# FFN up products by Strassen's algorithm in a two-layer diffusion step: seven block products in place of eight

## The chip, the cores and the metric

The kernel runs on 1 core of one Trainium2 chip. The metric is the device time of one execution in microseconds (us), taken as the median of several runs. PE is the matrix engine, DVE the vector engine, ACT the scalar engine, POOL the GpSimd engine, SP the engine whose queue issues most DMAs. SBUF is the on-chip memory that all engines read and write; PE writes its results to PSUM, which the code divides into buffers ("banks") of 512 fp32 columns and from which DVE and ACT read.

## What is computed

One inference step of two layers (shared structure, own weights) over 1152 tokens (128 context tokens, then 1024 latent ones) of width 1024. Each layer is a token mixer (three kinds of attention with one input and one output projection) and a gated convolutional FFN, each between norms whose scale, shift and gate (adaLN) are products of the conditioning vectors. What the change touches is the FFN:

```python
def conv_ffn(h, w_up, conv_w, conv_b, w_down):
    u = h @ w_up
    up = jnp.pad(u, ((0, 0), (1, 1), (0, 0)))
    u = up[:, :-2] * conv_w[0] + up[:, 1:-1] * conv_w[1] + up[:, 2:] * conv_w[2] + conv_b
    gate, val = jnp.split(u, 2, axis=-1)
    return (jax.nn.silu(gate) * val) @ w_down
...
    x = x + gt_m * rms_norm(o, g_post_mix)
    h = rms_norm(x, g_pre_ffn) * (1 + sc_f) + sh_f
    x = x + gt_f * rms_norm(conv_ffn(h, ffn_w_up, ffn_conv_w, ffn_conv_b, ffn_w_down), g_post_ffn)
```

`w_up` is 1024 x 5632, `w_down` 2816 x 1024. The context and the latent tokens are two sequences for the convolution.

## The kernel before

The tokens are nine tiles of 128. Every large product is of fp32 values in three passes: a value x is split into hi, rounded by a cast, and lo = x - hi (`split`, L195), and PE adds hi·hi, hi·lo and lo·hi. The cast is ACT's, the subtraction POOL's or DVE's. The tile framework schedules the instructions from the order in which the code issues them; each engine then runs its list in order and waits on semaphores. Buffers are taken from pools: a tag has a number of buffers, and a new tile waits for the last use of the buffer it gets; a pool that is opened in the room of an old one waits for that.

A layer has five stages. `phase_a` (L363) is the input projection, `phase_b` (L621) the attention, with its scores at L679 and its values at L727. `phase_c` (L944, stage C) is the output projection (L968), then per tile the norms (`norm_tiles`, L158: the product with the gate row at L166, the reciprocal root by Newton steps at L106 to L121, the scaling at L188) and the transposed, modulated and split h (`h_group`, L139) in groups of one to three tiles.

`phase_u` (L989, stage U) runs over 22 pairs f of a gate and a value block of 128 features. `load_w` (L342) loads a block of 512 KB, ACT casts it and POOL subtracts. `up_mm` (L998) makes the block in three PSUM banks: 8 slices of the 1024 input features, 3 passes, 3 chunks of 384 tokens, 72 matmuls, so 144 per f. The convolution of width 3 is applied to the blocks straight from PSUM: ACT writes the centre tap and the bias into `acc` (L1040), DVE adds the two shifted taps, with the product in PSUM as one input (`shifted`, L1015; 16 operations, since tokens are interleaved in groups of eight and chunks have edges). ACT applies SiLU to the gate (L1078), POOL multiplies gate and value (L1053), SP stores the result to DRAM (`GT`). For f = 0 the products of chunks 0 and 1 come first, 96 matmuls, since the last tiles' h is not there yet; `pend` holds the generators of the last norms.

Beside U's products `along` (L1056) advances a generator: `ada_dve` (L297), the adaLN products of this layer's last part and, in layer 0, of all the next layer's, as vector operations on DVE (L311, 512 wide) with a transpose on PE and a reduction (L321). U is followed by the class `Down` (L1095): per group of three tiles 22 blocks of `w_down`, loaded three ahead, 512-column matmuls into six banks (L1120). Its norms, one per tile, go along.

## Time and profile before

| | us |
|---|---|
| median of 3 runs | 3373.86 (3371.49 to 3375.37) |
| profiled execution, its own time | 3374.83 |
| its span in the profile | 3373.0 |
| PE busy | 3209.3 (95%) |
| DVE busy | 2165.7 (64%) |
| ACT busy | 1546.9 (46%) |
| POOL busy | 1127.5 (33%) |

The span runs from the first to the last instruction that the profile has; the device time has 1.8 us around it. Busy is the time in which an engine had an instruction at work; a busy PE is not necessarily PE at its peak. In rows of the timeline, consecutive instructions of a kind stand together with their count (x16), and a time in brackets is what the engine stood idle before them, with what ended that.

### The profile page before, as it was taken

The numbers are of one execution on the slowest core, as the hardware profiler recorded it, in microseconds if no ns is written. First come the engines' busy times: TensorE is split into PE (matmuls) and PEld (weight loads), VectorE is DVE, ScalarE is ACT, GpSimd is POOL, SyncE is SP. The second block draws the span as 40 slices with busy tenths as digits, with TensorE's granted clock in tenths as the row PEclk, the third lists the DMA queues.
The fourth block names the chain that finished last, engine by engine and source line by source line (L and its number), as shares of the span: only waits on it lengthen the run. The fifth ranks groups of instructions, "written<-read, shape, count | busy, mean of one in ns | idle before, by whom it ended". The sixth has DMA issues, their size and how long they took to land.

```text
span 3373.0 us, 51130 instructions
## 1 busy us (share of the span) xinstructions
PE 3209.3 (95%) x18068; PEld 2895.7 (86%) x18068; DVE 2165.7 (64%) x5367; ACT 1546.9 (46%) x3209; POOL 1127.5 (33%) x962
## 2 busy tenths in 40 slices
PE   8988999989999999999999899999899999999999
PEld 3868888877899999987788699888779999999887
DVE  5796788877788888435546728888777433333443
ACT  4321688875332222235544228888643222223443
POOL 2122345431233323344421314554313332323443
PEclk9999999999999999999999999999999999999999
DMA  6467431253243333255544563215423221123665
GB/s 238 132 182 224 140 77 40 66 168 132 80 140 123 122 120 120 79 187 191 192 137 126 150 189 87 59 41 133 158 94 100 87 73 65 65 69 118 207 204 167
DMA packets 224863, 428.78 MB, mean 127 GB/s; under 512 B 21088, under 2 KB 127456, under 8 KB 224608
## 3 DMA queue, kind: packets, MB, share of 16 engines
q1 hardware_dynamic: 223312, 424.33, 40.9%
q8 instruction: 143, 2.34, 0.3%
q10 hardware_dynamic: 1296, 1.19, 0.1%
q14 instruction: 112, 0.92, 0.1%
HBM read 324.05 MB, written 101.38 MB: 126 GB/s over the span
## 4 chain that ended last, share of the span: by engine, by line
PE 71%; DVE 13%; ACT 7%; issue 4%; DMA 3%; POOL 1%; SPq 0%; ACTq 0%; DVEq 0%; POOLq 0%
PE mm L1003 32%; PE mm L1120 15%; PE O L727 5%; PE T L709 4%; PE mm L968 4%; PE SA L679 4%; ACT P L689 3%; PE mm L591 2%; DVE PT L206 2%; ACT PT L205 2%; PE mm L375 1%; PE mm L376 1%; PE mm L374 1%; DVE nw_t L116 1%; PE SB L679 1%
## 5 line engine op out<-in xcount | busy, mean ns | idle before, releaser
L1003 PE MATMUL mm<-hhi,wu 128*128 128x384 f32 x4224 | 863.4, 335 | 3.1 <-POOL wu L200 2.2
L1003 PEld LDWEIGHTS mm<-hhi,wu 128*128 128x128 f32 x4224 | 742.7, 188 | 4.3 <-POOL wu L200 2.8
L1015 DVE SCALAR_TENSOR_TENSOR acc<-mm,conv,acc 128x336 f32<-128x336 f32 (+6 forms) x1408 | 412.5, 375 | 314.8 <-ACT acc L1040 314.5
L200 POOL TENSOR_TENSOR wu<-wraw,wu 128x1024 fp32r<-128x1024 f32 x123 | 302.2, 2458 | 690.3 <-ACT wu L197 690.2
L1003 PE MATMUL mm<-hlo,wu 128*128 128x384 f32 x2112 | 490.9, 334 | 0.0
L197 ACT CAST wu<-wraw 128x1024 fp32r<-128x1024 f32 x158 | 165.7, 1051 | 593.6 <-issue 369.6
L1003 PEld LDWEIGHTS mm<-hlo,wu 128*128 128x128 f32 x2112 | 377.1, 188 | 0.6 <-DVE hlo L153 0.4
L727 PE MATMUL O<-PT,V 128*128 128x256 f32 (+1 forms) x1936 | 334.4, 299 | 22.6 <-ACT PT L205 10.5
L698 POOL TENSOR_SCALAR P<-P,rs 128x1152 f32<-128x1152 f32 (+3 forms) x288 | 273.2, 950 | 185.5 <-DVE rs L697 123.0
L709 PE MATMUL T<-ident,P 128*128 128x128 f32 x1832 | 292.8, 278 | 16.5 <-DVE PT L206 12.3
L311 DVE SCALAR_TENSOR_TENSOR aacc<-wadv,sc,aacc 128x512 f32<-128x512 f32 x280 | 261.2, 976 | 63.5 <-DMA wadv<-w_ada 63.3
L206 DVE TENSOR_TENSOR PT<-T,PT 128x512 fp32r<-128x512 f32 (+1 forms) x448 | 284.4, 650 | 23.9 <-ACT PT L205 18.9
L727 PEld LDWEIGHTS O<-PT,V 128*128 128x128 f32 x1936 | 263.1, 192 | 40.2 <-ACT PT L205 16.7
L679 PE MATMUL SA<-k,q 128*128 128x256 f32 (+5 forms) x1224 | 283.8, 353 | 9.2 <-ACT ko L616 4.0
L1120 PE MATMUL mm<-wd,g 128*128 128x512 f32 x1224 | 288.1, 392 | 2.6 <-DVE wt L166 2.6
L1120 PEld LDWEIGHTS mm<-wd,g 128*128 128x128 f32 x1224 | 230.2, 189 | 51.4 <-DVE wt L166 3.5
L1120 PE MATMUL mm<-wu,g 128*128 128x512 f32 x1152 | 270.7, 391 | 2.6 <-DVE wt L166 2.6
L205 ACT CAST PT<-T 128x512 fp32r<-128x512 f32 (+1 forms) x448 | 241.9, 563 | 58.3 <-PE T L709 46.3
L1120 PEld LDWEIGHTS mm<-wu,g 128*128 128x128 f32 x1152 | 216.4, 188 | 48.2 <-DVE wt L166 3.5
L709 PEld LDWEIGHTS T<-ident,P 128*128 128x128 f32 x1832 | 210.4, 141 | 50.2 <-issue 17.6
L679 PEld LDWEIGHTS SA<-k,q 128*128 128x128 f32 (+1 forms) x1224 | 199.0, 193 | 32.9 <-ACT P L689 6.8
L702 DVE TENSOR_REDUCE mx<-SA 128x1 f32<-128x896 f32 (+1 forms) x192 | 182.4, 950 | 36.6 <-PE SA L679 36.6
(203 smaller groups left out, 5033.4 us busy)
## 6 DMA issues: line engine op xcount, KB each, us to landing
wraw<-w_down SPq DMA_DIRECT2D x132, 512.0 KB, 3.6
wraw<-w_up SPq DMA_DIRECT2D x88, 512.0 KB, 3.6
wadv<-w_ada SPq DMA_DIRECT2D x160, 256.0 KB, 3.0
GT<-acc SPq DMA_DIRECT2D x44, 576.0 KB, 3.0
graw<-GT SPq DMA_DIRECT2D x132, 192.0 KB, 3.1
...
```

Of the source, the lines that this page charges most:

```text
L200: (lo_eng or pool).tensor_tensor(out=lo, in0=raw, in1=hi.bitcast(F32), op=ALU.subtract)
L205: act.copy(hi, src)
L206: dve.tensor_tensor(out=lo, in0=src, in1=hi.bitcast(F32), op=ALU.subtract)
L311: dve.scalar_tensor_tensor(out=accs[i], in0=w, scalar=sc[:, k, i:i + 1], in1=accs[i], op0=ALU.mult, op1=ALU.add)
L679: pe.matmul(out, q[0:rows, qc:qc + 128], kview(k[0:rows]), start=(i == 0), stop=(i == len(passes) - 1))
L698: pool.tensor_scalar(out=P[:, :n], in0=P[:, :n], scalar1=rs, scalar2=1.0, op0=ALU.mult, op1=ALU.mult)
L702: dve.tensor_reduce(out=out, in_=src, op=ALU.max, axis=AX.X, negate=True)
L709: pe.transpose(tp[:, j * 128:(j + 1) * 128], p, ident)
L727: pe.matmul(op[0][:, c0:c1], V[:, vt, :], PT[e][:, sl, c0:c1], start=(i == 0 and e == 0), stop=(i == last and e == 1))
L1003: pe.matmul(pts[c][:, :CN], a[:, k, :], h_[:, k, c * CN:(c + 1) * CN], start=(k == 0 and a is whi and h_ is hhi), stop=(k == KC - 1 and a ...
L1015: dve.scalar_tensor_tensor(out=d, in0=src, scalar=w, in1=d, op0=ALU.mult, op1=ALU.add)
L1120: pe.matmul(pts[j], a[:, ts], d[:, 0, j * 512:(j + 1) * 512], start=(f == 0 and n == 0), stop=(f == NFF - 1 and n == 2))
```

## The change

For each f the products A·B, with A the two blocks (rows gate and value, columns the two halves of the 1024 input features) and B = h (rows the two halves of the features, columns the two halves of the tokens, 576 each), are made by the Strassen-Winograd scheme of seven products:

- of the weights: S1 = A21 + A22, S2 = S1 - A11, S3 = A11 - A21, S4 = A12 - S2 (class `Up`, `step`): S1 and S3 on POOL, S2 and S4 on DVE, 512 wide; the seven hi parts on ACT, the seven lo parts on POOL;
- of h: T3 = B22 - B12, T2 = T3 + B11, T1 = B22 - T2, T4 = B21 - T2, made once per layer (class `Halves`, `h_of`), tile by tile; T1, T4 and B22 go through DRAM;
- seven products A11·B11, A12·B21, S2·T2, S3·T3, A22·T4, S1·T1, S4·B22, each of 4 slices, 3 passes and 2 halves of 288 tokens: 24 matmuls, 168 per f, into a pair of PSUM banks `mm2` (three pairs);
- seven additions on DVE of a product in PSUM to a sum in SBUF (`add`, L1211), and a copy on ACT, which make `C0` (gate) and `C1` (value) in SBUF. The convolution's inputs are then both in SBUF (L1184): 8 operations of 1008, 112 and 15 elements per block. Gate and value of f - 1 are finished in f.

Besides: f = 0 has only A11·B11 and A12·B21 before it needs the last tile's h; `phase_c` has two pools of single buffers that alternate by tile, and h comes tile by tile (`SINGLE`); adaLN products are 256 wide, six steps per f, in U only this layer's last part and the next layer's first two parts, and the other three go along layer 0's Down (two steps per block); `Down` loads three ahead in the last layer and two in the first, `w_down` in two halves, the first two loads in U's buffers; the rope table and a gain row are loaded in `phase_a`; every pool has `reuse_waits="tile"`: a new tile waits for the last users of the tiles whose room it takes, and not for the whole old pool.

The diff, cut to its core:

```diff
-    const = ctx.enter_context(tc.tile_pool(name="const", bufs=1))
...
+    const = ctx.enter_context(tc.tile_pool(reuse_waits="tile", name="const", bufs=1))
...
+    def mm2():
+        return psum.tile([128, 1024], F32, name="mm2", tag="mm2", bufs=3)
...
+        (st0, p0), (st1, p1) = right("cp0"), right("cp1")
+        junk = p0.tile([128, 512], BF16, name="junk")
+        G = [gate_rows(z, 0, 0, p0.tile([128, D], F32, name="G")),
+             gate_rows(z, 0, 1, p1.tile([128, D], F32, name="G1"))]
...
+            xt = load_x(p, xin, t, "xt", 1)
+            wt = p.tile([128, D], F32, name="wt")
+            gens.append(norm_tiles(p, (t,), [pts.pop(t)], [[junk] * 2], [wt], [xt], G, xout, z.Af,
+                                   z.mods[:, 3], H, xs, SINGLE, (dve, dve), T.h_of))
...
+    HF, HT = KC // 2, NT // 2
...
+                B12, B22, B11, B21 = hr[:, 0:HF, n0:], hr[:, HF:KC, n0:], hs[:, 0:HF], hs[:, HF:KC]
+                dve.tensor_tensor(out=B12, in0=B22, in1=B12, op=ALU.subtract)
+                self.split("T3", r, B12)
+                dve.tensor_tensor(out=B11, in0=B12, in1=B11, op=ALU.add)
+                self.split("T2", r, B11)
+                pool.tensor_tensor(out=t1, in0=B22, in1=B11, op=ALU.subtract)
+                pool.tensor_tensor(out=B21, in0=B21, in1=B11, op=ALU.subtract)
...
+            self.raw = lambda n: p.tile([128, 1024], F32, name=n, bufs=1 if n == "A1" else 2)
+            self.sum = lambda n: p.tile([128, 512], F32, name=n)
+            self.hi = lambda n: p.tile([128, 512], F32R, name="h" + n)
+            self.lo = lambda n: p.tile([128, 512], F32R, name="l" + n)
...
+            if i == 0:
+                comb("S1", "A21", "A22", ALU.add, pool)
+                comb("S3", "A11", "A21", ALU.subtract, pool)
+                hi("A11")
+            elif i == 1:
+                comb("S2", "S1", "A11", ALU.subtract, dve)
+                lo("A11")
+                hi("A12")
+            elif i == 2:
+                comb("S4", "A12", "S2", ALU.subtract, dve)
+                lo("A12")
+                hi("S2")
+                lo("S2")
+            else:
+                n = ("S3", "A22", "S1", "S4")[i - 3]
+                hi(n)
+                lo(n)
+
+    def phase_u(l, z, T, W, p, up, pend, pend_done):
+
...
+        def product(s, t, f):
+            (shi, slo), (thi, tlo) = W.f[f][s], T.parts[t]
+            acc = mm2()
+            for k in range(HF):
+                for n, (a, b) in enumerate(((shi, thi), (shi, tlo), (slo, thi))):
+                    for j in range(2):
+                        pe.matmul(acc[:, j * 512:j * 512 + 288], a[:, k * 128:(k + 1) * 128],
+                                  b[:, k, j * 288:(j + 1) * 288], start=(k == 0 and n == 0),
+                                  stop=(k == HF - 1 and n == 2))
+            return acc
...
+            def add(d0, s0, n, te, fe):
+                d = dst[:, d0:d0 + n, te]
+                dve.scalar_tensor_tensor(out=d, in0=src[:, s0:s0 + n, fe], scalar=w, in1=d,
+                                         op0=ALU.mult, op1=ALU.add)
+
+            if sh == 1:
+                add(0, 0, 144, slice(1, 8), slice(0, 7))
+                add(1, 0, 15, 0, 7)
+                add(32, 16, 112, 0, 7)
+                add(17, 128, 15, 0, 7)
+            else:
+                add(0, 0, 144, slice(0, 7), slice(1, 8))
+                add(0, 1, 15, 7, 0)
+                add(16, 32, 112, 7, 0)
+                add(128, 17, 15, 7, 0)
+
...
+            act.activation(out=acc, in_=C, func=AF.Identity, scale=cw[:, 1:2], bias=cw[:, 3:4])
...
+            u2 = up.tile([128, HT], F32, name="U2")
+            a = product("A11", "B11", f)
+            act.copy(two(u2), view(a))
+            if f:
+                W.step(f, 6)
+                W.load(f + 1)
+                prep(0)
+                ag = conv(Cg, f - 1, 0)
+                act.activation(out=ag, in_=ag, func=AF.Silu)
+                pool.tensor_tensor(out=av, in0=ag, in1=av, op=ALU.mult)
+                nc.sync.dma_start(out=GT[l][f - 1], in_=av)
+                add(Cg[:, 0:HT], u2, product("A12", "B21", f))
+                prep(1)
+                along(2)
+                add(u2, u2, product("S2", "T2", f))
+                prep(2)
+                add(Cv[:, HT:], u2, product("S3", "T3", f))
             else:
...
+                a = product("A12", "B21", f)
                 for g in list(pend):
                     finish(g, pend)
+                T.from_last()
                 p, extra = pend_done()
-                up_mm(wg, pg, (2,))
-                up_mm(wv, pv_, (2,))
-            else:
-                up_mm(wg, pg, range(NCH))
-            ag = conv(pg, f, 0)
-            act.activation(out=ag, in_=ag, func=AF.Silu)
-            along()
-            if f > 0:
-                wv = load_up(f + NFF)
-                pv_ = [mm() for _ in range(NCH)]
-                up_mm(wv, pv_, range(NCH))
...
+            prep(3)
+            along(2)
+            add(Cv[:, 0:HT], Cv[:, HT:], product("A22", "T4", f))
+            prep(4)
+            a = product("S1", "T1", f)
+            add(Cv[:, HT:], Cv[:, HT:], a)
+            add(u2, u2, a)
+            prep(5)
+            av = conv(Cv, f + NFF, 1)
+            add(Cg[:, HT:], u2, product("S4", "B22", f))
+            along(2)
+        ag = conv(Cg, f, 0)
...
-                    self.load(i0 + f + AHEAD)
+                    self.load(i0 + f + self.bufs - 1)
...
+            ex.append(ada_dve(l, z, p, (5,), 256))
             if zn is not None:
-                ex.append(ada_dve(l + 1, zn, p, (1, 0, 2, 3, 4), 512))
...
+        extra = [] if zn is None else [ada_dve(l + 1, zn, ep, (2, 3, 4), 256)]
...
+        def step():
+            advance(gens)
+            for _ in range(2):
+                advance(extra)
```

What the order of the instructions shows, at three places.

DVE in U of layer 0, within one f. Before: a convolution's end (`mm` is the product in PSUM, `acc` the sum in SBUF), then an adaLN step (`aacc`).

```order
L1015 SCALAR_TENSOR_TENSOR acc_13006<-mm,conv,acc_13006 128x48x7 x2
L1015 SCALAR_TENSOR_TENSOR acc_13006<-mm,conv,acc_13006 128x48
L1015 SCALAR_TENSOR_TENSOR acc_13006<-mm,conv,acc_13006 128x32
L1015 SCALAR_TENSOR_TENSOR acc_13006<-mm,conv,acc_13006 128x15
L1015 SCALAR_TENSOR_TENSOR acc_13006<-mm,conv,acc_13006 128x48x7
L1015 SCALAR_TENSOR_TENSOR acc_13006<-mm,conv,acc_13006 128x48
L311 SCALAR_TENSOR_TENSOR aacc_12801<-wadv,sc,aacc_12801 128x512
L321 TENSOR_REDUCE ada_m<-aux 128x4
```

Now: additions of products (`C`, `U`, `S` and `A` are in SBUF), a weight combination and a convolution between adaLN steps.

```order
L1211 TENSOR_TENSOR C_10712<-C_10712,mm_14129 128x576
L313 SCALAR_TENSOR_TENSOR aacc_14119<-wadv,sc,aacc_14119 128x256
L313 SCALAR_TENSOR_TENSOR aacc_14120<-wadv,sc,aacc_14120 128x256
L313 SCALAR_TENSOR_TENSOR aacc_14119<-wadv,sc,aacc_14119 128x256
L313 SCALAR_TENSOR_TENSOR aacc_14120<-wadv,sc,aacc_14120 128x256
L1211 TENSOR_TENSOR C_10712<-C_10712,mm_14159 128x576
L1211 TENSOR_TENSOR U_13953<-U_13953,mm_14159 128x576
L1125 TENSOR_TENSOR S_14314<-S_14269,A_14265 128x512
L313 SCALAR_TENSOR_TENSOR aacc_14119<-wadv,sc,aacc_14119 128x256
L1184 SCALAR_TENSOR_TENSOR acc_14190<-C_10712,conv,acc_14190 128x144x7
L1184 SCALAR_TENSOR_TENSOR acc_14190<-C_10712,conv,acc_14190 128x15
L1184 SCALAR_TENSOR_TENSOR acc_14190<-C_10712,conv,acc_14190 128x112
```

The convolution reads SBUF twice where it read PSUM and SBUF, and the adaLN operations stand between the additions that free PSUM.

POOL in U, from one product of gate and value to the next. Before, the low parts of two blocks:

```order
L1053 TENSOR_TENSOR acc_12650<-acc_12536,acc_12650 128x1152
L200 TENSOR_TENSOR wu_12927<-wraw,wu_12926 128x1024
L200 TENSOR_TENSOR wu_13041<-wraw,wu_13040 128x1024
L1053 TENSOR_TENSOR acc_12891<-acc_12765,acc_12891 128x1152
```

Now seven low parts (L1133) and two combinations (L1125):

```order
L1225 TENSOR_TENSOR acc_12801<-acc_12894,acc_12801 128x1152
L1133 TENSOR_TENSOR lS_12979<-S_12933,hS_12977 128x512
L1133 TENSOR_TENSOR lS_13009<-S_12890,hS_13007 128x512
L1125 TENSOR_TENSOR S_13161<-A_13155,A_13156 128x512
L1133 TENSOR_TENSOR lA_13047<-A_12885,hA_13045 128x512
L1133 TENSOR_TENSOR lS_13078<-S_12888,hS_13076 128x512
L1125 TENSOR_TENSOR S_13159<-A_13156 128x512
L1133 TENSOR_TENSOR lS_13153<-S_12973,hS_13151 128x512
L1133 TENSOR_TENSOR lA_13206<-A_13155,hA_13163 128x512
L1133 TENSOR_TENSOR lA_13242<-A_13155,hA_13208 128x512
L1225 TENSOR_TENSOR acc_13080<-acc_13165,acc_13080 128x1152
```

Three instructions of POOL per f became ten.

PE at the start of U, layer 0. Before, at the transposes of the last tile's h (`wt`), 96 up products of chunks 0 and 1 lie between these rows and the last output projection:

```order
L1003 MATMUL mm<-hhi,wu_10474 128x384
L1003 MATMUL mm<-hlo,wu_10474 128x384
L1003 MATMUL mm<-hhi,wu_10475 128x384
L148 MATMUL aux<-ident,wt 128x128 x2
L1003 MATMUL mm<-hhi,wu_10465 128x384
```

Now the end of the second product (`hA`, `lA`), the first matmuls of S3·T3 and S2·T2, whose columns are there (`hS`), and the transposes of tile 8:

```order
L1164 MATMUL mm_10676<-hlo,hA_10518 128x288 x2
L1164 MATMUL mm_10676<-hhi,lA_10522 128x288 x2
L1164 MATMUL mm_10730<-hhi,hS_10528 128x288
L1164 MATMUL mm_10755<-hhi,hS_10524 128x288
L1035 MATMUL aux<-ident,wt 128x128 x8
L1164 MATMUL mm_10730<-hhi,hS_10528 128x288
L1164 MATMUL mm_10730<-hlo,hS_10528 128x288
```

Two products of 24 matmuls stand ahead of the transposes, where 96 longer ones did.

## Rows read from the trace of the kernel before

**Rows 1.** Windows: stretch, us; PE, PEld, DVE, ACT, POOL busy (count); PEclk, DMA, GB/s.

```profile
876.00:1442.70 566.70, 563.80 (x3283) 560.71 (x3282) 423.04 (x963) 159.02 (x225) 174.89 (x74) 1.00 0.36 114
1442.70:1760.00 317.30, 307.36 (x1361) 250.83 (x1360) 151.68 (x313) 150.29 (x250) 129.39 (x80) 0.99 0.58 184
2535.00:3092.80 557.80, 554.85 (x3201) 552.14 (x3200) 252.99 (x768) 158.53 (x224) 170.11 (x74) 1.00 0.23 78
```

**Rows 2.** Chain of waits: start us, us, what.

```profile
1442.71 89.82 PE mm L1120 x396
...
2638.33 454.48 PE mm L1003 x2622
```

**Rows 3.** Timeline of PE in attention: start us, us, engine, line, operation, count.

```profile
700.36 0.32 PE L727 MATMUL O<-PT,V 128*128 128x256 f32 x1
...
700.83 1.30 PE L727 MATMUL O<-PT,V 128*128 128x256 f32 x9
```

**Rows 4.** Groups by line and form: busy us, mean ns | idle before.

```profile
L1015 DVE SCALAR_TENSOR_TENSOR acc<-mm,conv,acc 128x336 f32<-128x336 f32 x352 | 190.3, 562 | 0.0
...
L1053 POOL TENSOR_TENSOR acc<-acc,acc 128x1152 f32<-128x1152 f32 x44 | 119.9, 2725 | 199.3 <-DVE acc L1015 176.2 <-issue 16.5 <-DMA wraw<-w_up 6.6
...
L1078 ACT ACTIVATE acc<-acc 128x1152 f32<-128x1152 f32 x44 | 51.5, 1170 | 173.0 <-DVE acc L1015 173.0
...
L166 DVE TENSOR_TENSOR wt<-mm,G 128x512 f32<-128x512 f32 x72 | 48.7, 686 | 39.6 <-ACT wt L127 31.2 <-ACT junk L127 8.3
...
L1015 DVE SCALAR_TENSOR_TENSOR acc<-mm,conv,acc 128x15 f32<-128x15 f32 x176 | 42.8, 243 | 0.0
...
L321 DVE TENSOR_REDUCE ada_m<-aux 128x4 f32<-128x512 f32 x40 | 27.5, 689 | 36.6 <-PE aux L320 36.2
...
L200 POOL TENSOR_TENSOR cv<-cv,cv 128x512 fp32r<-128x512 f32 x2 | 2.6, 1295 | 0.2 <-ACT cv L197 0.2
```

**Rows 5.** Timeline of DVE, in stage C and in U of layer 0.

```profile
857.40 1.29 DVE L166 TENSOR_TENSOR wt<-mm,G 128x512 f32<-128x512 f32 x2 [1.85 <-ACT wt L127]
...
1103.61 4.66 DVE L1015 SCALAR_TENSOR_TENSOR acc<-mm,conv,acc 128x127 f32<-128x127 f32 x16
1108.18 2.73 DVE L311 SCALAR_TENSOR_TENSOR aacc<-wadv,sc,aacc 128x512 f32<-128x512 f32 x4
```

**Rows 6.** Timeline of all engines at 1112 us, in U of layer 0.

```profile
1112.38 4.22 DVE L311 SCALAR_TENSOR_TENSOR aacc<-wadv,sc,aacc 128x512 f32<-128x512 f32 x3 [1.47 <-DMA wadv<-w_ada]
1112.54 2.85 POOL L200 TENSOR_TENSOR wu<-wraw,wu 128x1024 fp32r<-128x1024 f32 x1 [10.07 <-ACT wu L197]
```

**Rows 7.** Timeline of all engines at 1138 us, in U of layer 0.

```profile
1138.38 2.41 POOL L200 TENSOR_TENSOR wu<-wraw,wu 128x1024 fp32r<-128x1024 f32 x1 [10.97 <-ACT wu L197]
...
1138.85 2.29 DVE L1015 SCALAR_TENSOR_TENSOR acc<-mm,conv,acc 128x127 f32<-128x127 f32 x8 [1.59 <-ACT acc L1040]
```

**Rows 8.** Timeline of all engines at 859 us, in stage C of layer 0.

```profile
858.96 4.76 POOL L200 TENSOR_TENSOR wu<-wraw,wu 128x1024 fp32r<-128x1024 f32 x2 [8.91 <-ACT wu L197]
858.98 2.40 DVE L116 SCALAR_TENSOR_TENSOR nw_t<-nw_u,nw_v 128x1 f32<-128x1 f32 x1
...
861.41 2.33 DVE L120 SCALAR_TENSOR_TENSOR nw_u<-nw_t,nw_u 128x1 f32<-128x1 f32 x1
```

**Rows 9.** Timeline at the start of U, layer 0: the last tile's norm.

```profile
876.94 0.68 DVE L166 TENSOR_TENSOR wt<-mm,G 128x512 f32<-128x512 f32 x1
...
886.35 1.15 ACT L188 ACTIVATE wt<-xt,nw_u 128x1024 f32<-128x1024 f32 x1 [1.83 <-DVE nw_u L120]
```

**Rows 10.** DMA issues: KB each, median us from issue to landing.

```profile
GT<-acc SPq DMA_DIRECT2D x44, 576.0 KB, 3.0
```

**Rows 11.** Waits of PE from 730 to 880 us: us in total, times, longest.

```profile
PE O L727 <- DVE Y L734: 3.9, 2, 3.5
PE mm L968 <- ACT hhi L197: 2.0, 1, 2.0
```

More of the change, by code (lines that the diff above doesn't have):

```diff
@@ L38 @@
 GW = 64
+SINGLE = tuple((t,) for t in range(NTT))
 GROUPS = ((0,), (1, 2), (3, 4, 5), (6, 7), (8,))
@@ L165, in norm_tiles @@
             for j, wj in enumerate(halves(w[i])):
-                eng[j].tensor_tensor(out=wj, in0=src[i][j], in1=halves(G[:, 1 if tiles[i] == 0 else 0])[j],
+                eng[j].tensor_tensor(out=wj, in0=src[i][j], in1=halves(G[1 if tiles[i] == 0 else 0])[j],
                                      op=ALU.mult)
@@ L377, in project @@
             return pt
[L380 removed]
+        with tc.tile_pool(reuse_waits="tile", name="av", bufs=1) as p:
             for t in range(NTT):
@@ L1084, in phase_u @@
-            av = conv(pv_, f + NFF, 1)
-            gate(ag, av)
-            along()
+                Cg, Cv = [p.tile([128, NT], F32, name=f"C{j}") for j in range(2)]
+                add(Cg[:, 0:HT], u2, a)
+                W.load(f + 1)
+                prep(0)
+                prep(1)
+                b = product("S3", "T3", f)
+                add(u2, u2, product("S2", "T2", f))
+                prep(2)
+                add(Cv[:, HT:], u2, b)
+            prep(3)
+            along(2)
+            add(Cv[:, 0:HT], Cv[:, HT:], product("A22", "T4", f))
@@ L1242, in tile_kernel @@
             late_consts(l + 1, zn)
-        pend, cst = phase_c(l, z, Y, yst, H, xin, XD[2 * l], wp)
-        gst, dst, yst, G = ExitStack(), None, None, None
-        down = Down(l, wp, gst.enter_context(tc.tile_pool(name="gp", bufs=1)))
+        T = Halves(H, l)
+        wst, wp = left("cw")
+        pend, odd_done, all_done = phase_c(l, z, Y, yst, H, xin, XD[2 * l], wp, T)
+        wst.close()
+        ust, up = left("up")
+        W = Up(l, up)
+        W.load(0)
+        for i in range(7):
+            W.step(0, i)
@@ new lines, in tile_kernel @@
+        down = Down(l, 4 if zn is None else 3)
+        for i, (r, g, ns) in enumerate((("A1", "S1", ("A11", "A12", "S2")), ("A2", "S3", ("S3", "A22", "S1")))):
+            hi, lo = [W.hi(n) for n in ns], [W.lo(n) for n in ns]
+            down.load(i, (W.raw(r), hi[:2], lo[:2], W.sum(g), hi[2], lo[2]))
+        dst.close()
+        tst.close()
+        ust.close()
+        fst, down.p = left("wf")
+        down.load(2)
+        ast = ExitStack()
+        if zn is not None:
+            ast, wp = right("aw")
```

366 lines of the change are left out of this document (205 added, 161 removed).

## The prediction

> **What bounds the kernel now.** I read the windows by stage first. The FFN up stage, called U below, is 566.7 us in layer 0 and 557.8 us in layer 1, together a third of the span of 3373.0 us. PE is busy in 563.8 and 554.9 us of them at a granted clock of 1.00; DVE is busy 423.0 us in the first and 253.0 us in the second, POOL 174.9 and 170.1 us [rows 1]. The chain of waits says it more sharply: in U it is one run of PE matmuls after another, for instance 2622 of them in 454.48 us with nothing between, 173.3 ns for 384 columns. In the Down stage 396 matmuls of 512 columns take 89.82 us, 226.8 ns each [rows 2]. So U is bound by matmul columns and by nothing else: only a shorter PE stream, or a second engine that grows past it, changes its time. An f (one gate and one value block) costs 144 x 173.35 ns = 24.96 us.
>
> **PE, the term that is removed.** An f becomes 7 x 24 = 168 matmuls of 288 columns. No row has 288. From 384 (173.3) to 512 (226.8) a column costs 0.418 ns, which carried down gives 133.3 ns. On the other side lies a run of nine 256-column matmuls in 1.30 us; without about 0.30 for the last one's own length, 125 ns from start to start [rows 3], and interpolating from there to 384 gives 137 ns. So an f needs 168 x 133.3 = 22.4 us, at most 23.0; I take 22.4, because the long runs are the surer rows. Saved at most: 44 x 2.56 = 112 us. The Trainium skill (TensorE: Matmul & The Clock Gate, Back-to-back issue gap) gives columns / 2.4 + 2.5 ns at the full clock, an estimate of 122.5 ns at 288 and 20.6 us for an f; the same rule makes 162.5 ns of 384 columns where the rows have 173.3, so the rows decide. By it PE would be further below the other two engines, and the forecast would stay.
>
> **DVE, what is added.** Four scalar_tensor_tensor of 512 elements from SBUF take 2.73 us, 0.66 from start to start [rows 5]. From 15 to 336 elements the convolution's rows go from 243 to 562 ns [rows 4], 1.0 ns an element; so an operation occupies DVE for 1.0 ns an element and 0.15 us. Per f:
> - two convolutions, now from SBUF to SBUF, of 8 operations and 2300 elements each: 2 x (2.30 + 8 x 0.15) = 7.0 us (before, 16 operations in 4.66 us, twice [rows 5]);
> - two weight combinations of 512: two tensor_tensor of 512 take 1.29 us, one 686 ns, so 0.60 from start to start [rows 4, 5]: 1.2 us;
> - seven additions of 576 with one input in PSUM, as that row's: 7 x (0.60 + 0.06) = 4.6 us.
>
> Sum 12.8 us of 22.4. The adaLN vector products run along with six steps an f, now 256 wide: some 10.7 operations x 0.40 and a reduction (689 ns for 512 [rows 4]) make 4.7 us, so 17.5 us in such an f. By the order of DVE they fill f = 1 to 17 of layer 0 and f = 1 to 5 of layer 1.
>
> **POOL, what is added.** Seven low parts and two combinations of 512 at 1.295 us and one product of 1152 at 2.725 us [rows 4]: 9 x 1.295 + 2.725 = 14.4 us an f (before 2 x 2.4 [rows 7] + 2.7 = 7.5).
>
> **DVE and POOL together.** Neither alone reaches 22.4. But they do not run freely beside each other. With a POOL subtraction going, three L311 operations (both inputs in SBUF) take 4.22 us [rows 6] where 3 x 0.68 would be 2.05, and two one-element operations, L116 and L120, take 2.40 and 2.33 us, the length of the two POOL operations there [rows 8]. Eight L1015 operations, with one input in PSUM, take 2.29 us beside a POOL operation of 2.41 [rows 7], half of the 4.66 for 16. The change moves the convolution from the second kind to the first, and doubles POOL. Only the additions lie beside POOL for certain. Bounds: with only the data time of DVE's SBUF operations exclusive, (4.6 + 1.0) + 14.4 = 20.0 us, with adaLN + 10.7 x 0.256 = 22.8; with all but the additions exclusive, 12.8 + 14.4 - 4.6 = 22.6, with adaLN 17.5 + 9.8 = 27.3. A plain f can lose more by order: from the end of the sixth product (S1·T1) DVE owes two additions, a combination, a convolution and the seventh addition (1.3 + 0.6 + 3.5 + 0.7 = 6.1 us) before a pair of banks comes free. There are three pairs, so PE needs it three products, 9.6 us, later. Five POOL operations in between (5 x 1.16, their rows without the fixed part) make 11.9, 2.3 too late: 24.7. I take 23.0 for a plain f, nearer to PE's 22.4, since the first bound leaves slack, and 25.0 for one with adaLN, the middle of 22.8 and 27.3. Behind DVE's and POOL's queues only PE waits in U.
>
> **ACT and SP.** ACT has three operations of 1152 at 1.17 us [rows 4] and eight of 512 or 576, less each: below 13 us of 22.4, hidden. The weights' bytes are the same, and the gate's stores stay [rows 10]. The halves of the tokens go through DRAM on SP's queue in C, many tiles ahead of who reads them: 0, or 3 us if the last one is late, the landing time of such a transfer [rows 10].
>
> **The first f.** Before, 96 matmuls of chunks 0 and 1 (16.6 us) lay between the out-projection and the need for tile 8. Now only A11·B11 and A12·B21, 6.4 us, can go before the transposes of tile 8, as PE's order shows. The last norm's chain runs from L166 at 876.94 to the end of L188 at 886.35 + 1.15 [rows 9], 11.4 us after the stage's start at 876.1. Then come eight transposes and their evacuation (2 us), and subtract, split, add and split for T3 and T2 (3 to 3.5 us), with up to 4.7 us lost to POOL as in the stretch of L116 [rows 8]: products go on 16.5 to 20 us after the start, and five of them (16 us) follow. I take 36.5 us (32.5 to 42) for f = 0, against 24.96.
>
> **Elsewhere.** Down of layer 0 gets 84 us of adaLN on DVE (192 operations of 256 and 24 reductions); DVE has 151.7 and POOL 129.4 us there, of 317.3, PE 307.4 [rows 1]. 236 + 129 would be too much if nothing overlapped: +6 us (0 to +25). The waits by tile can only shorten seams: before one of them PE waits 3.9 us for DVE at L727 and 2.0 us for ACT at L968 [rows 11]. I take 0, at best -12, both in both layers.
>
> **Sum.** Layer 0: 36.5 + 17 x 25 + 4 x 23 = 553.5 for 566.7: -13.2. Layer 1: 36.5 + 5 x 25 + 16 x 23 = 529.5 for 557.8: -28.3. Down +6. Together -35 us from the profiled execution's 3374.83 (the span of 3373.0 and 1.8 around it; the median of the three runs, 3373.86, is 1.0 lower): **3340 us**.
>
> **Rivals.**
> 1. *DVE and POOL exclude each other and set U's pace: slower.* If DVE's operations stand behind POOL's nearly always, an adaLN f takes 26.5 us, a plain one 24, f = 0 takes 40 and Down +12. Layer 0: 40 + 17 x 26.5 + 4 x 24 = 586.5 (+20), layer 1: 40 + 5 x 26.5 + 16 x 24 = 556.5 (-1): +31, **3406**. At the worst ends (27.3, 24.7, 42, +25) it is about 3454. Above 26.6 us per adaLN f it decides, the other terms as forecast. For it: [rows 6, 8]; against it: 20 of the 44 f's have no adaLN, and 20.0 us of exclusive work fit there. The Trainium skill (SBUF — State Buffer, Who interferes with whom) has the rule: a DVE instruction with two SBUF inputs contends with a GpSimd one that reads SBUF, one with a single SBUF input does not, and the one that is late fully blocks for the other's whole instruction. The three rows agree with it, and by it this rival's terms are the likelier for the adaLN f's.
> 2. *PE bound everywhere.* DVE and POOL fit between the products: f = 0 takes 32.5, an adaLN f 22.8, a plain one 22.4, so 509.7 and 504.9; Down 0: -110, **3265**. For it: the bound of 20.0; against it: 22.8 is reached only if no operation of DVE ever stands still with its fixed part.
> 3. *No change that can be told.* Gains and losses are equal, with adaLN f's at about 26.6 us; or a 288-column matmul takes 24.96 / 168 = 148.6 ns, so that the columns saved go into a fixed cost. The rows at 256 and 384 [rows 2, 3] speak against the second.
>
> **How the numbers follow.** The forecast (U partly held by DVE and POOL) has 0.42; its own range is 3300 (24.0 per adaLN f, 22.7 plain, 34 for f = 0, Down 0) to 3368. Rival 2 has 0.18, rival 1 has 0.30, rival 3 has 0.10. About 0.2%, 6.7 us, is what a measurement of this kernel can tell from no change. Faster: 0.42 + 0.18 = 0.60; same 0.10; slower 0.30. The range reaches from rival 2's main case to somewhat above rival 1's, 3265 to 3420; it leaves out about 0.08 on each side.
>
> **What would show it.** In the windows of the changed kernel: U near 553 us in layer 0 and 530 in layer 1, and PE gaps in it that DVE's additions at L1211 end. In single steps: matmuls of 288 columns 133 to 137 ns from start to start; L1184 of 1008 elements near 1.2 us alone and over 2 us beside POOL; adaLN f's near 25.0 and plain ones near 23.0; a PE gap of some 10 us behind the first two products of each U. If PE runs through U without gaps, rival 2 holds; if adaLN f's take over 26.6 us, rival 1.

## The result and the profile after

The changed kernel takes 3630.4 us (median of four runs, 3624.3 to 3639.8) where the kernel before takes 3373.9: a ratio of 1.0763 with a 95% interval of 1.0746 to 1.0780, 256 us slower. The forecast was 35 us faster, and even the worst ends of the slower rival gave only 3454. The profiled execution took 3624.25 us with a span of 3622.4.

By stages, from a stage's first product to the next stage's first (Down of layer 1 to its own last product), in us; "adaLN f" is the mean of f = 1 to 17 of layer 0, "plain f" that of f = 8 to 20 of layer 1. The last columns are the device time and that of the kernel before on the same chip (the kernels below ran once each, the first two rows are medians).

| kernel | C, layers 0 / 1 | U, 0 / 1 | f = 0 | adaLN f | plain f | Down, 0 / 1 | us | before |
|---|---|---|---|---|---|---|---|---|
| before | 119.0 / 118.9 | 566.5 / 557.5 | 28.4 | 25.7 | 24.96 | 289.2 / 272.5 | 3373.9 | |
| changed | 135.0 / 138.1 | 659.2 / 615.8 | 50.6 | 29.6 | 25.8 | 352.4 / 284.7 | 3630.4 | 3373.9 |
| e1_lo_once | 137.5 / 138.5 | 545.6 / 533.7 | 52.4 | 23.7 | 22.4 | 356.5 / 284.2 | 3438.4 | 3371.8 |
| e2_p7_first | 135.4 / 136.1 | 632.0 / 576.6 | 52.5 | 28.4 | 23.8 | 356.0 / 285.4 | 3564.4 | 3371.8 |
| e3_ada_eighth | 135.6 / 137.8 | 601.0 / 597.2 | 50.5 | 26.4 | 25.8 | 315.0 / 288.5 | 3516.6 | 3371.8 |
| e4_lo_on_dve | 135.3 / 137.9 | 587.5 / 545.1 | 51.8 | 25.9 | 22.4 | 358.5 / 283.9 | 3486.5 | 3371.8 |
| e5_before_c_two_bufs | 117.4 / 118.3 | 567.1 / 557.9 | 28.5 | 25.8 | 24.96 | 287.8 / 272.5 | 3372.2 | 3366.6 |
| e6_best_parts | 134.2 / 138.5 | 592.4 / 543.2 | 51.1 | 26.2 | 22.5 | 300.8 / 285.1 | 3457.6 | 3366.6 |
| e7_before_reuse_tile | 119.3 / 119.7 | 566.6 / 557.0 | 28.4 | 25.7 | 24.96 | 289.1 / 272.6 | 3363.2 | 3366.6 |
| e8_before_ada_in_down | 119.0 / 119.5 | 561.0 / 557.6 | 28.4 | 25.5 | 24.96 | 335.5 / 272.6 | 3416.0 | 3366.6 |
| e9_c_lo_on_dve | 125.0 / 129.3 | 662.9 / 615.9 | 52.5 | 29.7 | 25.8 | 354.4 / 284.9 | 3614.7 | 3373.2 |
| e10_tail_lo_later | 138.6 / 138.3 | 658.3 / 615.8 | 52.3 | 29.4 | 25.8 | 353.4 / 284.6 | 3632.4 | 3373.2 |
| e11_best_parts_2 | 127.7 / 126.9 | 573.0 / 542.3 | 47.0 | 25.0 | 22.7 | 301.0 / 283.0 | 3415.9 | 3373.2 |
| e12_tail_no_lo | 135.4 / 140.3 | 655.3 / 611.6 | 46.9 | 29.6 | 25.8 | 355.5 / 285.8 | 3628.0 | 3368.9 |

So U lost 92.7 + 58.3 us, Down 63.2 + 12.2, C 16.0 + 19.2; the input projections and attention gained 13.5. That is 248 of the 249 us between the two spans; the rest lies behind Down's last product.

The windows of the changed kernel: U of layer 0, then of layer 1 (columns as in [rows 1]).

```profile
891.00:1550.00 659.00, 549.88 (x3756) 535.77 (x3756) 573.44 (x804) 197.01 (x268) 354.40 (x229) 0.92 0.26 81
...
2713.00:3329.00 616.00, 529.80 (x3725) 518.71 (x3725) 458.30 (x650) 199.37 (x269) 345.30 (x229) 0.94 0.23 73
```

Against [rows 1], PE is no longer busy through U: 549.9 of 659.0 us, at a granted clock of 0.92 instead of 1.00. DVE went from 423.0 to 573.4 us in layer 0 and POOL from 174.9 to 354.4. Who PE waits for is in its waits over the whole span (us in total, times, longest):

```profile
PE mm L1164 <- DVE C L1211: 115.8, 68, 6.0
PE aux L1035 <- ACT wt L201: 50.1, 16, 10.4
PE mm L1164 <- DVE U L1211: 36.7, 17, 3.9
PE aux L322 <- DVE aacc L313: 16.3, 10, 3.5
```

152.5 us of waits in U end with an addition of DVE, 50.1 are waits for the normed tile before its transposes, and 16.3 are for adaLN sums. What DVE's adaLN steps cost is in its groups by line, over the whole span (us busy, mean ns | idle before):

```profile
L313 DVE SCALAR_TENSOR_TENSOR aacc<-wadv,sc,aacc 128x256 f32<-128x256 f32 x392 | 309.5, 832 | 48.3 <-DMA wadv<-w_ada 48.0
```

One by one in U of layer 0, the 100 of 192 such steps that meet no POOL operation take 457 ns on average, and the 92 that do take 1356.

The place within a plain f is in the timeline of DVE, POOL and PE in layer 1, from the end of the sixth product on (other rows left out):

```profile
3018.47 0.76 DVE L1211 TENSOR_TENSOR C<-C,mm 128x576 f32<-128x576 f32 x1 [2.44 <-PE mm L1164]
...
3019.96 1.30 POOL L1133 TENSOR_TENSOR lS<-S,hS 128x512 fp32r<-128x512 f32 x1
3021.34 1.30 POOL L1125 TENSOR_TENSOR S<-A 128x512 f32<-128x512 f32 x1
3022.58 1.31 POOL L1133 TENSOR_TENSOR lS<-S,hS 128x512 fp32r<-128x512 f32 x1
3022.68 1.77 DVE L1125 TENSOR_TENSOR S<-S,A 128x512 f32<-128x512 f32 x1 [2.79 <-POOL S L1125]
3024.37 4.77 DVE L1184 SCALAR_TENSOR_TENSOR acc<-C,conv,acc 128x1008 f32<-128x1008 f32 x8
...
3029.07 0.74 DVE L1211 TENSOR_TENSOR C<-U,mm 128x576 f32<-128x576 f32 x1
...
3029.95 0.51 PE L1164 MATMUL mm<-hhi,hS 128*128 128x288 f32 x2 [1.92 <-DVE C L1211]
```

The addition that frees the seventh product's banks ends at 3029.81, 11.3 us after the sixth product (the prediction had worked out 11.9 against 9.6 of cover), and PE stands still for 1.92. That the two sums are so close is partly luck, for the parts are others: DVE waits 2.79 us for POOL's S1, which stands behind low parts in POOL's list, the combination S2 takes 1.77 instead of 0.68 beside a POOL operation, and the convolution 4.77 (3.79 in an undisturbed stretch). After the gap PE also runs slower for a while, as three windows in a row of the same f's show:

```profile
3025.00:3031.00 6.00, 4.08 (x31) 3.87 (x30) 5.41 (x10) 1.33 (x3) 1.48 (x1) 1.00 0.00 0
3031.00:3037.00 6.00, 6.00 (x35) 6.00 (x35) 5.08 (x9) 1.59 (x3) 1.85 (x1) 0.72 0.23 70
3037.00:3043.00 6.00, 6.00 (x47) 6.00 (x46) 2.73 (x4) 2.52 (x4) 5.05 (x3) 1.00 0.29 115
```

Behind the gap the granted clock is 0.72 on average over 6 us, a mix of the levels of 1.2 and 2.4 GHz, and PE, busy throughout, starts 35 matmuls where the next window has 47. Most plain f's alternate between 26.05 us (PE idle once, for 1.92, and such a stretch) and 25.48 (idle twice, for 1.62 and 0.98, and hardly a slow matmul). From start to start that is 22.4 + 2.1 for the gap + 1.6 for slow matmuls, and 22.4 + 1.8 + 1.1 + 0.2. A gap of 1.92 us is not always followed by a slow stretch: f = 18 of layer 1 has one and none. What decides it stays open.

### The profile page after: what moved, and what is told of

Read it like the earlier page. It is cut to its first block, busy times and chain, and to the rows that moved or that the text cites. A ratio compares the mean times of both kernels' runs of the same rounds, so it can differ in the third digit from the quotient of the medians.

```text
span 3622.4 us, 54770 instructions
## 1 busy us (share of the span) xinstructions
PE 3201.5 (88%) x19124; PEld 2854.4 (79%) x19124; DVE 2673.0 (74%) x5395; ACT 1652.3 (46%) x3469; POOL 1516.0 (42%) x1332
## 5 line engine op out<-in xcount | busy, mean ns | idle before, releaser
L1184 DVE SCALAR_TENSOR_TENSOR acc<-C,conv,acc 128x1008 f32<-128x1008 f32 (+1 forms) x704 | 442.6, 701 | 47.3 <-ACT acc L1201 47.3
L313 DVE SCALAR_TENSOR_TENSOR aacc<-wadv,sc,aacc 128x256 f32<-128x256 f32 (+1 forms) x476 | 372.5, 821 | 67.4 <-DMA wadv<-w_ada 67.0
L1133 POOL TENSOR_TENSOR lA<-A,hA 128x512 fp32r<-128x512 f32 x132 | 197.0, 1495 | 299.7 <-ACT hA L1129 292.3
L722 PE MATMUL T<-ident,P 128*128 128x128 f32 x1832 | 292.1, 277 | 16.2 <-DVE PT L219 12.2
L1303 PE MATMUL mm<-dh,gh 128*128 128x512 f32 x768 | 255.2, 404 | 20.7 <-DVE wt L179 12.0
L1133 POOL TENSOR_TENSOR lS<-S,hS 128x512 fp32r<-128x512 f32 x176 | 247.0, 1414 | 58.9 <-ACT hS L1129 58.6
L213 POOL TENSOR_TENSOR dl<-draw,dh 128x512 fp32r<-128x512 f32 x128 | 173.9, 1378 | 230.8 <-ACT dh L210 227.2
L1303 PE MATMUL mm<-dl,gh 128*128 128x512 f32 x768 | 254.1, 402 | 9.3 <-POOL dl L213 6.1
L1164 PE MATMUL mm<-hhi,hS 128*128 128x288 f32 x704 | 169.1, 324 | 96.3 <-DVE C L1211 81.5
L1303 PE MATMUL mm<-dh,gl 128*128 128x512 f32 x768 | 251.0, 399 | 0.0
L722 PEld LDWEIGHTS T<-ident,P 128*128 128x128 f32 x1832 | 209.7, 141 | 50.1 <-issue 18.3
L1201 ACT ACTIVATE acc<-C,conv 128x1152 f32<-128x1152 f32 x88 | 119.0, 1352 | 192.8 <-DVE C L1211 189.6
L210 ACT CAST dh<-draw 128x512 fp32r<-128x512 f32 x256 | 146.5, 617 | 129.7 <-DMA draw<-w_down 117.7
```

Source lines behind the costliest of these rows:

```text
L313: dve.scalar_tensor_tensor(out=accs[i], in0=w, scalar=sc[:, k, i:i + 1], in1=accs[i], op0=ALU.mult, op1=ALU.add)
L722: pe.transpose(tp[:, j * 128:(j + 1) * 128], p, ident)
L1133: eng.tensor_tensor(out=w[n][1], in0=x[n], in1=w[n][0].bitcast(F32), op=ALU.subtract)
L1164: pe.matmul(acc[:, j * 512:j * 512 + 288], a[:, k * 128:(k + 1) * 128], b[:, k, j * 288:(j + 1) * 288], start=(k == 0 and n == 0), stop=(k ...
L1184: dve.scalar_tensor_tensor(out=d, in0=src[:, s0:s0 + n, fe], scalar=w, in1=d, op0=ALU.mult, op1=ALU.add)
L1303: pe.matmul(pts[j], a[:, ts], d[j], start=(f == 0 and n == 0), stop=(f == NFF - 1 and n == 2))
```

## The experiments

Each is an edit of the changed kernel, or of the kernel before where its name says so.

**POOL's low parts made once.**

```diff
             def lo(n, eng=pool):
+                if f:
+                    w[n][1] = self.f[0][n][1]
+                    return
                 w[n][1] = self.lo(n)
```

> The changed kernel, with POOL's seven low parts of the weights made for f = 0 only and used again in every later f (the low parts of the other blocks are left out). POOL's work in U falls from 14.4 to about 5.3 us an f; DVE's list and PE's list stay as they are. Theory A (DVE's SBUF-to-SBUF operations and POOL's exclude each other, and that pushes the seventh product's addition, which stands behind the convolution, past the 9.6 us that the three bank pairs give): a plain f (25.8 us in the changed kernel) falls to 22.2 to 23.0, an adaLN f (29.4) to 24 to 26, the run to 3500 to 3540 us. Theory B (DVE's own amount and order of work is enough, POOL plays no part): plain f's stay at 25 to 26, adaLN f's at 29, the run stays within 20 us of 3624.

Plain f's take 22.40 us, each of them, 168 matmuls of 133.3 ns: PE bound, as the first term of the prediction had it. The adaLN f's fall to 23.7. U loses 113.6 and 82.1 us, 196 of the 249 us. Its windows (U of layer 0, U of layer 1):

```profile
893.00:1437.00 544.00, 510.62 (x3746) 504.88 (x3746) 461.82 (x802) 199.74 (x269) 144.12 (x82) 0.97 0.32 99
...
2607.00:3141.00 534.00, 503.12 (x3707) 499.88 (x3708) 379.78 (x653) 203.84 (x274) 140.65 (x82) 0.97 0.27 86
```

DVE's list is the same as in the changed kernel, and its busy time still falls from 573.4 to 461.8 us: 112 us of it were spent standing behind POOL. Theory A holds, theory B falls, though the gain is larger than theory A's figures: adaLN f's of 24 to 26 us and a run of 3500 to 3540 had been expected, and 23.7 and 3438.4 came. The clock rises to 0.97 with it, by an edit of POOL's list alone, so the low clock went with the gaps and was not their cause.

**The seventh addition ahead of the convolution.**

```diff
-            av = conv(Cv, f + NFF, 1)
             add(Cg[:, HT:], u2, product("S4", "B22", f))
+            av = conv(Cv, f + NFF, 1)
```

> The changed kernel, with one pair of statements swapped: the addition of the seventh product stands ahead of the value convolution on DVE instead of behind it. Nothing else changes. Theory A (what PE waits for is the order: the convolution, stretched by POOL, ahead of an addition that frees banks): the gap after the second product of an f is gone or below 0.3 us, a plain f falls from 25.8 to 23.0 to 24.3, the run by 40 to 70 us. Theory B (DVE and POOL together have too much work in an f, wherever it stands): the gap comes back at another product, plain f's stay above 25.3 and the run within 15 us of 3624.

The gap behind the second product is gone in plain f's, which take 23.6 to 23.9 us; one behind the fourth product, 1.1 to 1.6 us of PE idle, remains. The run is 60 to 66 us shorter. The order is worth 2 us in a plain f and 1.2 in an adaLN f; the 1.4 us that a plain f is still above 22.4 go in the runs that relieve POOL.

**One of eight adaLN steps.** `ada_dve` gets an argument, 1 in U and Down:

```diff
                 for k in range(KC):
+                    if k >= kn:
+                        yield
+                        continue
```

> The changed kernel, with only the first of eight vector-product steps of each adaLN block in U and in Down (seven eighths of those products are left out); the steps keep their places and the transposes and reductions stay. Theory A (the adaLN operations on DVE, blocked by POOL, cost both stages their time): the f's 1 to 17 of layer 0 become plain ones, 25.8 us instead of 29.4 on average, so U of layer 0 falls by 50 to 65 us and that of layer 1 by 15 to 20; Down of layer 0 falls from 352 us to 290 to 305. Theory C (Down of layer 0 is slow because it loads only two blocks ahead, in halves, and its traffic is late): Down of layer 0 stays above 335 us.

The adaLN f's fall by 3.2 us to 26.4, nearly a plain one, and Down of layer 0 by 37.4 to 315.0, between the two theories' figures for Down: adaLN is most of it, not all. U of layer 0 falls by 58.

**Low parts and combinations on DVE.**

```diff
-            def lo(n, eng=pool):
+            def lo(n, eng=dve):
...
-                comb("S1", "A21", "A22", ALU.add, pool)
-                comb("S3", "A11", "A21", ALU.subtract, pool)
+                comb("S1", "A21", "A22", ALU.add, dve)
+                comb("S3", "A11", "A21", ALU.subtract, dve)
```

> The changed kernel, with the seven low parts and both combinations that POOL made moved to DVE; POOL keeps only the product of gate and value in U. DVE's own work in a plain f rises from 12.8 to 18.2 us. Theory A (exclusion): what counts is the sum of both engines' exclusive work, which falls from 22.6 to about 16 + 2.7, so a plain f falls from 25.8 to 22.3 to 23.8; an adaLN f with 22.9 us of DVE's own work is 24 to 27, the run 3490 to 3560. Theory B (DVE's own amount and order): plain f's grow to 27 or more, adaLN f's to 31 or more, the run to over 3670 us.

Nothing is left out here, DVE has 5.4 us more to do in every f, and the run is 144 us shorter than the changed kernel's, just below the 3490 to 3560 expected: plain f's take 22.40 us without a gap. Groups by line, of DVE in this run, then of POOL and DVE in the changed kernel:

```profile
L1184 DVE SCALAR_TENSOR_TENSOR acc<-C,conv,acc 128x15 f32<-128x15 f32 x352 | 79.9, 249 | 0.0
```

```profile
L1133 POOL TENSOR_TENSOR lS<-S,hS 128x512 fp32r<-128x512 f32 x176 | 247.0, 1414 | 58.9 <-ACT hS L1129 58.6 <-PE aux L322 0.3
...
L1184 DVE SCALAR_TENSOR_TENSOR acc<-C,conv,acc 128x15 f32<-128x15 f32 x352 | 153.3, 456 | 0.0
```

The 15-element shifts cost 249 ns without POOL's company, as in [rows 4] (243), and 456 with it. The additions at L1211, with one input in PSUM, are the control: in U of layer 0 of the changed kernel they take 744 ns apart from POOL's operations and 748 beside them. POOL pays too: 1414 ns for what took 1295. The adaLN f's are now bound by DVE's own work, 12.8 + 5.4 + 4.7 = 22.9 us, and POOL's product of 2.7: 25.6, measured 25.9, with DVE busy in 25.4 of them. What e1 and e4 take away together is both the exclusion and the wait for S1 in POOL's list; the row with 2.79 us above shows that the second is a part.

**Stage C with two buffers, in the kernel before.**

```diff
-            xt = load_x(p, xin, t, "xt", 4)
-            wt = p.tile([128, D], F32, name="wt", bufs=5)
+            xt = load_x(p, xin, t, "xt", 2)
+            wt = p.tile([128, D], F32, name="wt", bufs=2)
...
-                                   z.mods[:, 3], H, xs, GROUPS, (dve, dve)))
+                                   z.mods[:, 3], H, xs, tuple((i,) for i in range(NTT)), (dve, dve)))
```

> The kernel before, with stage C as the change has it in its buffers alone: h made tile by tile instead of in groups, and two buffers each for the residual and the norm's work tile instead of four and five. No Strassen, no halves of the tokens. In the changed kernel stage C takes 135.0 and 138.1 us where it took 119.0 and 118.9. Theory D (with two buffers the norm's chain of one tile holds back the next but one, and PE waits for its transposes): stage C grows to 128 to 140 us in both layers and the run by 15 to 45 us, with PE waits for the scaling at L188. Theory E (it is the work that the halves add in C: sums, splits and DRAM copies on DVE, ACT and POOL): stage C stays at 119 to 123 us, the run within 8 us of 3373.

C stays at 117.4 and 118.3 us: theory D falls, and theory E is left, which this run does not test by itself. In the changed kernel's C the timeline of DVE and POOL shows something else:

```profile
818.70 3.64 DVE L188 SCALAR_TENSOR_TENSOR xt<-wt,nw_u,xt 128x512 f32<-128x512 f32 x2
818.74 2.39 POOL L213 TENSOR_TENSOR hlo<-hr,hhi 128x1024 fp32r<-128x1024 f32 x1 [7.65 <-DVE nw_u L133]
...
832.01 2.39 POOL L213 TENSOR_TENSOR hlo<-hr,hhi 128x1024 fp32r<-128x1024 f32 x1 [10.89 <-ACT hhi L210]
832.11 2.31 DVE L129 SCALAR_TENSOR_TENSOR nw_t<-nw_u,nw_v 128x1 f32<-128x1 f32 x1
```

h's low part is one POOL operation of 1024 elements per tile now, and the next tile's norm stands behind it: L188 takes 3.64 us where it takes 1.41 elsewhere, a one-element operation 2.31 us. That is [rows 8] again, in a place where the prediction had not looked.

**The low part of h on DVE.**

```diff
-                split(hr[:, :, :n0], *[x[:, :, cs] for x in H])
+                split(hr[:, :, :n0], *[x[:, :, cs] for x in H], lo_eng=dve)
```

> The changed kernel, with one argument changed in stage C: the low part of each tile's h in the first half of the tokens, one operation of 1024 elements, is made by DVE and not by POOL. Theory A (that operation of 2.39 us holds up the next tile's norm on DVE, and PE waits for its transposes): stage C falls from 135.0 and 138.1 us to 122 to 130, the waits of PE before the transposes of tiles 1 to 4 fall from 0.9 to 3.6 us to below 1.5, the run by 12 to 30 us. Rival (the eight transposes of a tile stand too early in PE's order, whatever POOL does): stage C stays at 132 us or more.

C falls by 10.0 and 8.8 us to 125.0 and 129.3. In layer 0 PE's waits in C for the normed tile fall from 15.6 us in seven to

```profile
PE aux L1035 <- ACT wt L201: 6.6, 5, 2.8
```

so theory A holds for about half of C's loss, though the longest wait left is 2.8 us, not below 1.5. The 6 to 10 us a layer that stay were not tried. In layer 0 PE then stands 6.2 us for the normed tiles of the second half, 3.2 for the output projection's weights, and 2.8 at C's end for the first hi part of U's weights, 12.2 in all, where the kernel before has 6.7.

**adaLN in Down, in the kernel before.**

```diff
-                ex.append(ada_dve(l + 1, zn, p, (1, 0, 2, 3, 4), 512))
+                ex.append(ada_dve(l + 1, zn, p, (1, 0), 512))
...
+        extra = [] if zn is None else [ada_dve(l + 1, zn, ep, (2, 3, 4), 256)]
+        def step():
+            advance(gens)
+            for _ in range(2):
+                advance(extra)
...
-        down.run(tile_done, lambda: advance(gens), lambda: more_w0((0, 1)), 4 if zn is None else 2)
+        down.run(tile_done, step, lambda: more_w0((0, 1)), 4 if zn is None else 2)
```

> The kernel before, with the adaLN products of layer 1's parts 2 to 4 in layer 0's Down, 256 wide and two steps a block as in the change, instead of in U. Down keeps its loads three ahead. Theory A (the adaLN operations on DVE, exclusive with POOL, are what slows Down): Down of layer 0 grows from 289.2 to 315 to 335 us, U stays at 566 as it is bound by PE, and the run grows by 25 to 45 us. Theory C (the change's Down is slow because of its loads: two ahead, in halves): Down of layer 0 stays below 300 us and the run within 10 us of 3372.

Down of layer 0 goes from 289.2 to 335.5 us and the run is 49.4 us longer: this move alone is 46 of the 63 us, at the upper end of theory A's figure. The 49.4 us are against a run of the kernel before on the same chip and above the 25 to 45 expected; against the profiled run above it is 41, as U gets 5.5 us shorter. PE's largest wait there and DVE's largest group in that window:

```profile
PE aux L320 <- DVE aacc L311: 11.5, 4, 5.9
```

```profile
L311 DVE SCALAR_TENSOR_TENSOR aacc<-wadv,sc,aacc 128x256 f32<-128x256 f32 x168 | 121.7, 770 | 31.9 <-DMA wadv<-w_ada 31.6
```

A 256-wide step takes 770 ns, nearly twice the 0.40 us that I had put, DVE stands 31.6 us for the weights' DMA, and since each engine runs its list in order, the low parts and norms behind it come late, and PE's transposes of the sums wait ahead of products.

**Every pool by tile, in the kernel before** (`reuse_waits="tile"` in each `tile_pool`).

> The kernel before, with every pool's reuse by tile instead of by pool and nothing else. Forecast: 0 to -12 us, at the seams alone. Theory: the input projection and attention of layer 1, 684.5 us before and 672.7 in the changed kernel, take 673 to 679, since the seams between Down, the input projection and the attention are freed: the run 4 to 12 us shorter. Rival: those 12 us come from where the rope table and the gain row are loaded, and the run stays within 3 us of 3372.

3.4 us shorter than the kernel before on its chip, a single run each: of the size forecast (0 to -12), just under the theory's 4 and beside the rival's 3. The run's time does not tell the two apart, but the stage does: the input projection and attention of layer 1 take 676.2 us, inside the theory's 673 to 679, where e5 and e8, on the same chip without this edit, take 684.8 and 683.9. So the waits by tile give about 8 of the 12 us there.

**Late parts of the first f later in the code** (steps 3 to 6 of f = 0 issued behind the last tile's h).

> The changed kernel, with four of the seven low parts of the first weight block (S3, A22, S1, S4) made by POOL behind the last tile's h instead of ahead of it. Theory A (these four operations, 4.92 us in a row, hold up the last norm's Newton steps on DVE): the first f falls from 50.6 and 50.7 us to 43 to 47 in both layers, the run by 7 to 15 us. Rival (two products cannot cover the last norm's chain in any case, and the parts made late cost what they gave): the first f stays at 49 to 52 us.

No change, 52.3 and 50.7 us for f = 0. But it tested nothing: the framework's schedule put POOL's four operations where they had been.

```profile
905.83 4.92 POOL L1133 TENSOR_TENSOR lS<-S,hS 128x512 fp32r<-128x512 f32 x4
```

**The same parts not made.**

```diff
             def lo(n, eng=pool):
+                if f == 0 and i > 2:
+                    w[n][1] = w[n][0]
+                    return
```

> The changed kernel, with four of the first weight block's low parts in each layer (S3, A22, S1, S4 of f = 0) not made: their products take the hi part in their place, so that part of f = 0 is left out. In the run that only placed these four later in the code, POOL still did them at the same time, between the last norm's Newton steps. Theory A (POOL's operations hold up the last norm): the first f falls from 50.6 and 50.7 us to 44 to 47.5, PE's gap of 17 us to 11 to 14. Rival (the length of the chain itself, with two products to cover it): the first f stays at 49 to 52 us.

f = 0 falls to 46.9 and 46.7 us. In the changed kernel the last norm's steps beside POOL, and PE's wait (PE at the end):

```profile
901.30 4.92 POOL L1133 TENSOR_TENSOR lS<-S,hS 128x512 fp32r<-128x512 f32 x4
901.39 1.19 DVE L133 SCALAR_TENSOR_TENSOR nw_u<-nw_t,nw_u 128x1 f32<-128x1 f32 x1
...
912.40 1.97 PE L1035 MATMUL aux<-ident,wt 128*128 128x128 f32 x8 [10.34 <-ACT wt L201]
```

Without them such a step takes 0.16 us, and PE's wait of 10.34 us is 6.45:

```profile
904.56 0.16 DVE L133 SCALAR_TENSOR_TENSOR nw_u<-nw_t,nw_u 128x1 f32<-128x1 f32 x1
...
911.59 1.97 PE L1035 MATMUL aux<-ident,wt 128*128 128x128 f32 x8 [6.45 <-ACT wt L201]
```

So the exclusion by these four is 3.9 us of the first f's loss of 22. The other 18 are not divided by any run. The length of the chain with two products to cover it is a part, but so is more of the same exclusion: in this run seven of DVE's 512-wide operations in f = 0 still take 1.70 to 2.19 us (0.68 elsewhere), with POOL's combinations and low parts beside them. The clock is a third: in the changed kernel it is 0.72 on average over f = 0.

**What helped, together.** Low parts on DVE, the seventh addition first, layer 1's adaLN parts in its input projection:

> The changed kernel with three changes at once: low parts and combinations of the weights on DVE (as in the run before), the seventh product's addition ahead of the value convolution, and the adaLN products of layer 1's parts 2 to 4 taken out of layer 0's Down and into layer 1's input projection, where layer 0 has its own. The run with the low parts on DVE alone took 3486.5 us. Theory A: Down of layer 0 falls from 358 to 315 to 322, the input projection of layer 1 grows by 10 to 27, the adaLN f's of U fall from 25.9 to 24 to 25.5, plain ones stay at 22.4: 3425 to 3470 us, still over the 3373 of before, because C, the first f's and the rest of Down are untouched. Rival: the adaLN products cost in layer 1's input projection what they cost in Down, and the run stays at 3475 to 3500.

3457.6 us, inside the expected range: Down of layer 0 takes 300.8, less than the 315 to 322 expected, and the input projection and attention of layer 1 take 26 us more than in the changed kernel (698.7 against 672.7). The adaLN f's are a miss: 26.2 us, where 24 to 25.5 had been expected from 25.9. With h's low part on DVE, the late parts moved and five adaLN steps per f:

> All that helped so far in one kernel: low parts and combinations of the weights on DVE, the seventh product's addition ahead of the convolution, layer 1's adaLN parts 2 to 4 in its input projection (3457.6 us together), and now the low part of h in stage C on DVE, the first f's late parts behind the last tile, and five adaLN steps an f instead of six. Theory A: stage C about 125, the first f's 44 to 47, the adaLN f's 25 to 26: 3405 to 3440 us, still above the kernel before. Below 3367 would mean that the first f's and stage C hold more than the traces show.

3415.9 us, inside the expected range and 43 above the kernel before on its chip. U's f's 1 to 21 are now 12 and 33 us faster than before ((573.0 - 47.0) against (566.5 - 28.4), and the same for layer 1); the first f's give back 37, C 17, Down 22, layer 1's input projection 11. No version of the changed kernel beat the kernel before.

## Why the prediction was wrong

- *PE, 22.4 us an f*: right. Wherever nothing else held PE up, an f took 22.40 us, 133.3 ns a matmul. The row at 512 and the line through it carried over; the formula of the Trainium skill (TensorE: Matmul & The Clock Gate, Back-to-back issue gap), which is given there for an isolated matmul, an estimate of 20.6 us, did not.
- *DVE's and POOL's own work, 12.8 and 14.4 us*: right enough: with little of POOL beside it (e1) DVE is busy 13.9 us in a plain f, POOL 14.7 in the changed kernel's; e4 moved 5.4 us between them and the sum 25.6 met 25.9.
- *A plain f, 23.0*: 25.8, 16 of them in layer 1 and 4 in layer 0, 64 us over (20 of these in f = 6 of layer 1 and f = 18 of layer 0, 34.6 and 31.6 us, which still hold the end of the adaLN work). The chain to the seventh addition was in the text, with 24.7, and was the right one. The step that failed is the choice of 23.0 by the bound of 20.0: a sum of work says nothing of an engine that stands in order behind a wait. DVE's wait for POOL's S1, 2.79 us, I had no term for, nor for the 1.6 us of slow matmuls after a gap.
- *An adaLN f, 25.0, at most 27.3*: 29.6, 22 of them, 100 us over, the largest part. The step that failed is the middle taken between 22.8 and 27.3, as if half of the exclusive work overlapped. In f = 1 to 17 of layer 0 DVE is busy 26.6 us an f, its own work and its standing behind POOL, near the bound with all but the additions exclusive: a 256-wide step, put at 0.40, takes 832 ns, though alone it is 457, since an operation that meets POOL's waits for it however small it is. [Rows 8] had shown that, on one element. The other 2.9 us of an f DVE stands idle, in the 17 f's 18.3 us for POOL's S1, 11.6 for the adaLN weights' DMA, 9.1 for ACT and 8.7 for PE; the bound has no term for these.
- *f = 0, 36.5 (32.5 to 42)*: 50.6 and 50.7, 28 over. Two steps failed. The products went on 28.1 us after the start instead of 16.5 to 20 (the prediction's own terms, with the 4.7 for POOL, make 21.6): the 11.4 us chain of tile 8 was read where no chain of the tile ahead and no low parts lay in its way. And the products behind it took 22.5 us instead of 16, with gaps and a granted clock of 0.85 in that stretch.
- *Down, +6 (0 to +25)*: +63 and +12. The step that failed is the overlap: 84 us of adaLN on DVE were taken to disappear beside PE's 307 but for 6. In e8 this move alone cost 46 us, and a step took 770 ns where the 84 had 400. The +12 in both layers comes at the start, where the third block's loads stand behind the last f's convolution and gate; PE is idle there for 7.8 and 7.1 us. That is read from the trace and was not tried.
- *C, nothing*: +16 and +19. The prediction moved no term into C, though the low part of h is in the diff. e9 shows about half of it; the rest stays open.
- *Waits by tile, 0 to -12*: right in size; e7 has some 8 us of it in layer 1's input projection and attention.

The slower rival was the right mechanism with 0.30 and a price of +31: the exclusion holds, and the Trainium skill's rule (SBUF — State Buffer, Who interferes with whom), that the port pair which the two engines share is an exclusive lock, agrees with the two-microsecond rows of one element. It was undersized because its main case still let some of the work overlap, its worst case let DVE never stand idle, it was kept nearly all inside U, and nothing was added for a clock that falls when PE waits. Without POOL's low parts U is 545.6 and 533.7 us, a gain of 45 in all; with them it is a loss of 151.
